# Eight pairs of feature blocks with seven products, and the down projection split into an early and a late part

## The chip, the core and the metric

The kernel runs on one core of one Trainium2 chip. The metric is the device time of one execution in microseconds (us). The kernel before took 1034.69 us (median of 3 runs, 1034.62 to 1034.87).

## What is computed

The reference is one inference step of a decoder layer: two recurrent branches (mLSTM and retention), a gated merge and an output projection, a layer norm, a SwiGLU feed-forward network, and a second layer norm. There are 512 prompt tokens with outputs and 8 running sequences, so the feed-forward part works on 520 token columns; the model is 1024 wide and the feed-forward part 2816.

```python
def swiglu(x, w_gate, w_up, w_down):
    return (jax.nn.silu(x @ w_gate) * (x @ w_up)) @ w_down
...
        mix, ml_s, rt_s = token_mix(x, pos, run, ml_states[l], rt_states[l], w_in[l], b_in[l],
                                    ml_norm_g[l], rt_norm_g[l], w_out[l])
        x = layer_norm(ALPHA * x + mix, ln1_g[l], ln1_b[l])
        x = layer_norm(ALPHA * x + swiglu(x, w_gate[l], w_up[l], w_down[l]), ln2_g[l], ln2_b[l])
```

The 8 sequences also have matrix states (4 heads, two branches: 64 blocks), each of which is decayed, gets an outer product added and is written out.

## The kernel before

**Numbers as pairs.** Every float32 operand of a large matrix product is split into a rounded high part and the rest (`wH`/`wL`, `x1H`/`x1L`, `hH`/`hL`). ScalarE (ACT) rounds, VectorE (DVE) subtracts. A product of two tiles is then three matmuls into PSUM (low by high, high by low, high by high). All arrays are feature-major: tokens lie along the free axis, 520 columns worked as two halves of 260 ("A" and "B").

**Weights** arrive as 154 units of 128x1024 floats through SyncE's DMA queue (`load_units`, L168) into three `raw` buffers. `split_units` makes `wH` and `wL` in three buffers each; `prep` (L196), called in the middle of each step, starts the split of the unit that is used three steps later and then issues the next loads. The last six units have `wH`/`wL` storage of their own beside that: three of them get a `wy` buffer, the other three wait until `wH` is free.

**The order is written by hand.** Each engine works through its own list in the order in which the program issues it. `run_step` (L200) issues the matmuls of one unit (48 matmuls: 8 feature tiles, 3 parts, 2 halves); `run_pair` (L227) those of one half with one or two columns of units. PSUM tiles `pp` come from a pool of two. What reads a finished `pp` (its "evacuation", `drv["evac"]`) is issued at the start of the next group by `flush()`; helpers that have a second stage put it into `pending`, and `tick()` issues it two feature tiles later. A `side` function, called every two feature tiles, adds small work at counted places.

**Feed-forward part.** The first 4 of 22 feature blocks go by halves (`run_pair`), blocks 4 and 5 go as `plain`: a gate step (sigmoid times itself to `gt`) and an up step (times `gt`, split into `hH`, `hL`, row i). Blocks 6 to 13 go as four pairs in `quad` (L1437): two gate steps, then the two up blocks as one 2x2 by 2x2 block product with **seven** products of a quarter of the size instead of eight. Sums of the activations for that (`combine`, L1402) lie in rows 14 to 21 of `hH`/`hL`, which are not yet in use; sums of the weights are made on DVE from `raw` (`sums`), split (`wzH`/`wzL` for the first sum), and the results are put together on DVE (`post`, `times`, `row`). Blocks 14 to 21 are `plain` again.

**Down projection.** 8 output blocks j, 22 feature rows each, in units of 8, 8 and 6 rows. Blocks 0 to 5 go over both halves; blocks 6 and 7 go as a pair over half A, then block 6 over half B, then block 7 over half B, so that the second layer norm of half A runs beside half B. Evacuation: `z = ALPHA*z + pp` and a running sum `Ssum` over blocks. For half B a mean over blocks 0 to 6 is taken early (`seven`, L1617: a product with `ones7`), and what block 7 adds is corrected at the end.

**Beside it**: `upd_at(rate)` (L1326) is called every two feature tiles and starts state blocks at a rate `R` (L1336): a broadcast load `uk`, a load `uC` (3 blocks ahead, 5 buffers), two ACT and two DVE operations, and a store. All of these DMAs are issued by GpSimd (POOL). When all 64 are out, the pool `dq` is released and `kv_load` (L680) loads the saved operands of two heads, whose state products fill TensorE (PE) at the very end.

The start of a step in `run_step`, and the places of small work and the first two products in `quad`:

```python
        if st.first:
            tick()
            flush()
            drv["ps"] = pmain.tile([128, 2, 512], F32, name="pp")
...
        side = each(upd_at(R[2]), at_q({
            0: [sp(0, a, lambda: r0[:, a])],
            3: [sums],
...
            6: [lambda: tt(r0[:, a], r0[:, a], r1[:, b], ALU.add), sp(0, b, lambda: r0[:, a])],
...
        products = [
            (0, a, x(0, tA), aux, post("p1", None, None)),
            (0, b, y(1), aux, post("u", "p1", ALU.add)),
```

Here `sp` splits a half (a or b, 512 columns) of a weight sum, and the second product needs the half that is made in place 6 of 15.

In the layer norm `centre` subtracts the mean (DVE) and squares (ACT), `fold` adds squares (the first three on POOL, the rest on DVE), `token_cols` sums over partitions with small matmuls, `root` takes the power -0.5 on POOL (tile `nr`), and `over_tokens` spreads it with five transposes on PE. `steps(gen, when)` lists at which `side` count each stage is issued.

Of the kernel before, what the change touches and what calls it, by code (L numbers as in the profile page):

```python
# [25 lines left out]
FF = 22  # L26
# [55 lines left out]
def body(nc, tc, a, o):  # L82
# [1487 lines left out]
    for i in range(3):  # L1570
        extra[UL + i] = lambda: (wy.tile([128, 1024], F32R, name="wyH"), wy.tile([128, 1024], F32R, name="wyL"))
    for j in range(6):
        if j == 5:
            assert upd["n"] == len(UPD) and not pending
            dqp.release()
            kvp = tc.alloc_tile_pool(name="kvp", bufs=1)
            kvx = [kv_load(kvp, 0)]
        k0 = 0
        for n in (8, 8, 6):
            ks = [(k0 + i, slice(i * 128, (i + 1) * 128)) for i in range(n)]  # L1580
            run_step(Step(unit, ks, rhs_h, full, k0 == 0, n == 6, ev_d(j)), upd_at(R[4]))
            k0 += n
# [5 lines left out]
    def ev_pair(ps):
        stt(z[:, 6:8, sA], z[:, 6:8, sA], ALPHA, ps[:, :, :260], ALU.mult, ALU.add)
        add_sum(6, sA)  # L1590
        add_sum(7, sA)

# [21 lines left out]
    def seven():  # L1617
# [12 lines left out]
        tail["sq"] = sq  # L1630
# [103 lines left out]
def _pack(inp):  # L1734
# [26 lines left out]
    for i in range(0, FF, 2):  # L1761
        gu = [unit(w[:, 128 * j:128 * (j + 1)]) for j in (i, i + 1) for w in (wgt, wup)]
        units += [gu[n] for n in ((0, 2, 1, 3) if i in QUADS else (0, 1, 2, 3))]
    for j in range(8):
        k0 = 0
        for n in (8, 8, 6):
            units.append(unit(wd[k0 * 128:(k0 + n) * 128, 128 * j:128 * (j + 1)]))
            k0 += n

    units[-6:] = [units[-6 + 3 * (i % 2) + i // 2] for i in range(6)]  # L1770
    cs, dtab, rw, rs = _constants()
# [65 lines left out]
```

## Time and profile before

| | |
|---|---|
| median of 3 runs | 1034.69 us |
| the profiled execution, its own time | 1035.39 us |
| its span (first to last instruction) | 1033.3 us |
| mean granted TensorE clock | 0.999 |
| PE busy | 1024.7 us, 99% |
| DVE / ACT / POOL busy | 640.8 / 480.9 / 255.6 us |
| moved by DMA | 176.64 MB, 171 GB/s on the mean |

In rows of the timeline the first number is the start in us from the span's start, the second the duration, then engine, line and operation, the tiles written and read, and in brackets how long the engine had been idle before and what released it. L101, L104 and L98 are helpers, so groups are told apart by their tiles.

### The profile page before, as it was taken

To read this page: it belongs to the slowest core of one execution; us is meant where nothing else is said; L and a number is where in the kernel's file an instruction comes from. 1 tells how busy PE (TensorE), PEld (TensorE's weight loads), DVE (VectorE), ACT (ScalarE), POOL (GpSimd) and SP (SyncE) were. 2 spreads that over 40 slices of the span, in tenths; PEclk is the share of its full clock that TensorE was granted. 3 is DMA by queue.
4 is the path that set the end of the run, shared out by engine and by line. 5 is a ranking of instruction groups with operands and counts; after the bars stand their busy time and mean duration, and the time that the engine had idled before them with its cause. 6 is when DMAs were issued, how large, how long until landed. Compare 5 with 4: busy or idle time off the path is not lost.

```text
span 1033.3 us, 21326 instructions
## 1 busy us (share of the span) xinstructions
PE 1024.7 (99%) x8506; PEld 1017.9 (99%) x8506; DVE 640.8 (62%) x1423; ACT 480.9 (47%) x960; POOL 255.6 (25%) x431
## 2 busy tenths in 40 slices
PE   9999999999999999999999999999999999999998
PEld 8999999999999999999999999999999999999997
DVE  4747753568555486535595748768888655555345
ACT  5454443554424544435554316645544544444224
POOL 1212302312303232021122135321211333343004
PEclk9999999999999999999999999999999999999999
DMA  6334442544343754422345563364565878888633
GB/s 238 98 130 138 153 154 96 173 143 140 135 143 117 257 164 140 153 96 78 131 150 170 170 227 114 113 222 146 161 208 189 277 258 250 271 291 310 220 110 104
DMA packets 64715, 176.64 MB, mean 171 GB/s; under 512 B 9220, under 2 KB 18948, under 8 KB 64360
## 3 DMA queue, kind: packets, MB, share of 16 engines
q1 hardware_dynamic: 47080, 123.55, 34.7%
q0 software_dynamic: 17536, 51.74, 16.1%
q8 instruction: 67, 1.10, 0.4%
q14 instruction: 32, 0.26, 0.1%
HBM read 146.09 MB, written 27.85 MB: 168 GB/s over the span
## 4 chain that ended last, share of the span: by engine, by line
PE 91%; DVE 4%; issue 1%; ACT 1%; DMA 1%; POOL 1%; SPq 0%; POOLq 0%; DVEq 0%; ACTq 0%
PE pp L220 64%; PE pp L243 11%; PE aux L1541 2%; PE acc L1541 2%; PE aux L586 2%; PE acc L184 1%; PE acc L186 1%; PE acc L185 1%; DVE wL L101 1%; PE aux L184 1%; PE aux L185 1%; PE aux L186 1%; PE pp L350 1%; PE aux L826 1%; ACT wH L98 1%
## 5 line engine op out<-in xcount | busy, mean ns | idle before, releaser
L220 PE MATMUL pp<-xH,wL 128*128 128x260 f32 (+1 forms) x1248 | 259.4, 289 | 0.0
L220 PE MATMUL pp<-xH,wH 128*128 128x260 f32 (+1 forms) x1248 | 252.6, 284 | 0.0
L220 PE MATMUL pp<-xL,wH 128*128 128x260 f32 (+1 forms) x1248 | 252.4, 284 | 0.0
L101 DVE TENSOR_TENSOR wL<-raw,wH 128x1024 fp32r<-128x1024 f32 (+2 forms) x161 | 182.1, 1133 | 68.2 <-ACT wH L98 67.0
L220 PEld LDWEIGHTS pp<-xH,wL 128*128 128x128 f32 x1248 | 193.0, 189 | 0.7
L220 PEld LDWEIGHTS pp<-xH,wH 128*128 128x128 f32 x1248 | 193.0, 188 | 0.0
L220 PEld LDWEIGHTS pp<-xL,wH 128*128 128x128 f32 x1248 | 192.9, 188 | 0.0
L98 ACT ACTIVATE wH<-raw 128x1024 fp32r<-128x1024 f32 (+2 forms) x161 | 155.2, 966 | 42.6 <-PE pp L220 25.0
L220 PE MATMUL pp<-x1H,wL 128*128 128x260 f32 x448 | 90.2, 282 | 0.4 <-DVE gt L101 0.4
L220 PE MATMUL pp<-x1H,wH 128*128 128x260 f32 x448 | 90.3, 283 | 0.0
L220 PE MATMUL pp<-x1L,wH 128*128 128x260 f32 x448 | 90.1, 283 | 0.0
L220 PEld LDWEIGHTS pp<-x1H,wL 128*128 128x128 f32 x448 | 69.1, 189 | 0.7 <-DVE gt L101 0.7
L220 PEld LDWEIGHTS pp<-x1H,wH 128*128 128x128 f32 x448 | 69.1, 188 | 0.0
L220 PEld LDWEIGHTS pp<-x1L,wH 128*128 128x128 f32 x448 | 68.9, 188 | 0.0
L98 ACT ACTIVATE raw<-pp,cols 128x536 f32<-128x536 f32 (+1 forms) x48 | 33.7, 702 | 74.4 <-PE pp L220 69.3
L98 ACT ACTIVATE sq<-uk,vsA 128x256 f32<-128x256 f32 x128 | 56.9, 496 | 20.5 <-DMA uk<-kq3m 9.6
L104 DVE SCALAR_TENSOR_TENSOR dt<-dC,dq 128x256 f32<-128x256 f32 x128 | 57.4, 449 | 2.8 <-DMA dC<-sC 0.3
L220 PE MATMUL pp<-hH,wL 128*128 128x260 f32 x264 | 53.3, 283 | 0.0
L220 PE MATMUL pp<-hH,wH 128*128 128x260 f32 x264 | 53.1, 282 | 0.0
L220 PE MATMUL pp<-hL,wH 128*128 128x260 f32 x264 | 53.1, 282 | 0.0
L101 DVE TENSOR_TENSOR gt<-gt,pp 128x520 f32<-128x520 f32 (+1 forms) x44 | 26.2, 595 | 35.1 <-ACT gt L98 22.6
L98 ACT ACTIVATE tmp<-pp,cols 128x520 f32<-128x520 f32 (+1 forms) x25 | 16.7, 674 | 61.8 <-PE pp L220 61.8
(425 smaller groups left out, 2165.8 us busy)
## 6 DMA issues: line engine op xcount, KB each, us to landing
raw<-wall SPq DMA_DIRECT2D x154, 512.0 KB, 3.8
dC<-sC SPq DMA_DIRECT2D x32, 256.0 KB, 4.3
dC<-sS SPq DMA_DIRECT2D x32, 256.0 KB, 4.2
uC<-sC POOLq DMA_DIRECT2D x32, 256.0 KB, 6.2
dC<-uC POOLq DMA_DIRECT2D x32, 256.0 KB, 4.3
uC<-sS POOLq DMA_DIRECT2D x32, 256.0 KB, 6.0
dS<-uC POOLq DMA_DIRECT2D x32, 256.0 KB, 4.3
raw<-xT SPq DMA_DIRECT2D x8, 268.0 KB, 4.3
```

What stands on the lines that cost most here:

```text
L98: A.activation(out, in_, func, **kw)
L101: (eng or V).tensor_tensor(out, x, y, op=op)
L104: V.scalar_tensor_tensor(out, x, s, y, op0=op0, op1=op1, **kw)
L184: PE.matmul(out, ll, rh, start=start, stop=False)
L185: PE.matmul(out, lh, rl, start=False, stop=False)
L186: PE.matmul(out, lh, rh, start=False, stop=stop)
L220: PE.matmul(ps[:, hi, :wd], w, r[:, lo:lo + wd], start=(st.first and i == 0 and pi == 0), stop=(st.last and i == n - 1 and pi == 2))
L243: PE.matmul(ps[:, hi, :n], w[:, c], r, start=(i == 0 and pi == 0), stop=(i == last and pi == 2))
L350: PE.matmul(first_ps[u][:, hi, :268], w[:, c], r[:, k, hi * 268:(hi + 1) * 268], start=(k == 0 and pi == 0), stop=(k == 7 and pi == 2))
L586: PE.transpose(ps[:m, i * 256 + dt * 128:i * 256 + dt * 128 + 128], src[:, dt, 128 * j:128 * j + m], ident)
L826: PE.transpose(ps[:, 128 * i:128 * (i + 1)], tiles[h]["nat" + br][:, i, et * 128:(et + 1) * 128], ident)
L1541: PE.matmul(ps[:, :260], w[:, s], r, start=(k == 0 and pi == 0), stop=(k == 3 and pi == 2))
```

## The change

Four more pairs go with seven products: `QUADS` now covers blocks 6 to 21, and no block after 5 is `plain`. The sums of the activations must therefore stay in rows 14 to 21 of `hH`/`hL` to the end of block 21. Rows of blocks 14 to 21 are stored in rows 0 to 7 instead (`hrow`), and those are free because the down projection of feature rows 0 to 7 is done early: right after the pair of blocks 8 and 9, eight steps (one for each j, 48 matmuls, one unit) put `z = ALPHA*z + pp`. The down projection after the last pair then has 14 rows left for each j, in units of 6 and 8 rows, and adds `pp` to `z`. Blocks 0 to 4 go over both halves; block 5 now goes alone over half A, blocks 6 and 7 as a pair over half A, then 5, 6 and 7 each over half B. For half B the early mean is over blocks 0 to 5 (`six`, at other counts), and the sum of blocks 6 and 7 (`z67`) is corrected at the end. The rates `R` of the state updates change, so that all 64 are out before block 4 of the down projection.

```diff
-QUADS = range(6, 14, 2)
+QUADS = range(6, 22, 2)
+EARLY = 8
+HR = 14
...
+    def hrow(i):
+        return i if i < HR else i - HR
...
-    R = (0.33, 0.2, 0.19, 0.36, 0.44)
+    R = (0.35, 0.25, 0.21, 0.48, 0.56)
...
-            split(hH[:, i, :], hL[:, i, :], g)
+            split(hH[:, hrow(i), :], hL[:, hrow(i), :], g)
...
     for i in QUADS:
         quad(i)
-    for i in range(QUADS.stop, FF):
-        plain(i, upd_at(R[3]))
-    unit = UF + 2 * FF
+        if i == EARLY:
+            for j in range(8):
+                run_step(Step(UF + 2 * i + 4 + j, kcols, rhs_h, full, True, True, ev_early(j)), upd_at(R[3]))
+    unit = UF + 2 * FF + 8
...
-    for j in range(6):
-        if j == 5:
+    krows = (range(EARLY, HR), range(FF - HR))
+    for j in range(5):
+        if j == 4:
             assert upd["n"] == len(UPD) and not pending
             dqp.release()
             kvp = tc.alloc_tile_pool(name="kvp", bufs=1)
             kvx = [kv_load(kvp, 0)]
...
     split_units(NU - 1)
     load_units(NU)
     split_units(NU)
     drain()
     kvx.append(kv_load(kvp, 1))
-    run_pair(ks, rhs_h, 0, 260, ev_pair)
+    run_pair(down_ks(5), rhs_h, 0, 260, ev_rest(sA, 5))
+    run_pair(down_ks(6, 7), rhs_h, 0, 260, ev_rest(sA, 6, 7))
...
     def ev_six(ps):
-        stt(z[:, 6, sB], z[:, 6, sB], ALPHA, ps[:, 0, :260], ALU.mult, ALU.add)
-        add_sum(6, sB)
+        tt(z[:, 6, sB], z[:, 6, sB], ps[:, 0, :260], ALU.add)
+        sq[6] = bt.tile([128, 260], F32, name="sq", bufs=8)
+        act(sq[6], z[:, 6, sB], AF.Square)
+        tail["z67"] = bt.tile([128, 260], F32, name="sq", bufs=8)
+        tt(tail["z67"], z[:, 6, sB], z[:, 7, sB], ALU.add)
...
-    side = each(steps(lnA, (3, 4, 5, 7, 12, 15, 17)), steps(seven(), (13, 14, 15, 18)))
-    run_pair([(k, ws[:1]) for k, ws in ks], rhs_h, 260, 260, ev_six, side)
+    side = each(steps(lnA, (3, 4, 5, 7, 12, 15, 17)), steps(six(), (8, 9, 11, 15)))
+    run_pair(down_ks(5), rhs_h, 260, 260, ev_rest(sB, 5), side)
+    run_pair(down_ks(6), rhs_h, 260, 260, ev_six, side)
     last_ps = {}
-    run_pair([(k, ws[1:]) for k, ws in ks], rhs_h, 260, 260, lambda ps: last_ps.update(ps=ps), side)
+    run_pair(down_ks(7), rhs_h, 260, 260, lambda ps: last_ps.update(ps=ps), side)
...
     tt(z7, z7, last_ps["ps"][:, 0, :260], ALU.add)
-    sq4 = tail["sq"][4]
+    z67 = tail["z67"]
+    tt(z67, z67, last_ps["ps"][:, 0, :260], ALU.add)
...
-    token_cols(z7, pc)
+    token_cols(z67, pc)
     token_cols(sq7, pv2)
```

On the matmuls the change is a count: PE has 48 matmuls of 260 columns fewer (128x3 fewer in up steps, 7x12 for each of four pairs more). Where instructions change places is seen at three spots.

**DVE at the end of the down projection.** The list of DVE before; `uC` rows are state updates, `wL`/`wyL` rows splits of weight units (the last six are the last six units), `z<-z,pp` with 520 columns the evacuation of a whole output block, `128x2x260` that of the pair 6 and 7 over half A:

```order
L104 SCALAR_TENSOR_TENSOR uC<-uC,sq 128x256 x2
L101 TENSOR_TENSOR wL<-raw,wH 128x1024 x3
L104 SCALAR_TENSOR_TENSOR z<-z,pp 128x520
L101 TENSOR_TENSOR Ssum<-Ssum,z 128x520
L101 TENSOR_TENSOR wL<-raw,wH 128x1024
L101 TENSOR_TENSOR wyL<-raw,wyH 128x1024 x3
L101 TENSOR_TENSOR wL<-raw,wH 128x1024 x3
L104 SCALAR_TENSOR_TENSOR z<-z,pp 128x520
L101 TENSOR_TENSOR Ssum<-Ssum,z 128x520
```

The same place after the change:

```order
L104 TENSOR_TENSOR z<-z,pp 128x520
L104 TENSOR_TENSOR Ssum<-Ssum,z 128x520
L107 SCALAR_TENSOR_TENSOR uC<-uC,sq 128x256 x4
L104 TENSOR_TENSOR wL<-raw,wH 128x1024 x2
L104 TENSOR_TENSOR z<-z,pp 128x520
L104 TENSOR_TENSOR Ssum<-Ssum,z 128x520
L104 TENSOR_TENSOR wyL<-raw,wyH 128x1024 x3
L104 TENSOR_TENSOR wL<-raw,wH 128x1024 x3
L104 TENSOR_TENSOR z<-z,pp 128x520
L104 TENSOR_TENSOR Ssum<-Ssum,z 128x520
L104 TENSOR_TENSOR z<-z,pp 128x260
```

In both lists the last full block is evacuated behind the splits of all six last units; that block is now block 4 instead of 5, with the 260 columns of block 5 behind it, and the last updates stand one block of weights nearer to it: two updates behind the evacuation of block 2, where before one stood behind that of block 3.

**DVE beside half B.** Before; `z<-z,aux` is the subtraction of a mean, `sq<-sq` the folding of squares, `vc` the small column that `root` reads:

```order
L104 SCALAR_TENSOR_TENSOR z<-z,pp 128x2x260
L101 TENSOR_TENSOR Ssum<-Ssum,z 128x260 x2
L101 TENSOR_TENSOR z<-z,aux 128x260 x8
L101 TENSOR_TENSOR sq<-sq 128x260 x4
L104 SCALAR_TENSOR_TENSOR z<-z,pp 128x260
L101 TENSOR_TENSOR Ssum<-Ssum,z 128x260
L110 TENSOR_SCALAR vc<-aux 52x5
L104 SCALAR_TENSOR_TENSOR z<-z,aux 128x260
L101 TENSOR_TENSOR z<-z,aux 128x260 x4
```

And after the change:

```order
L104 TENSOR_TENSOR z<-z,pp 128x2x260
L104 TENSOR_TENSOR Ssum<-Ssum,z 128x260 x2
L104 TENSOR_TENSOR z<-z,aux 128x260 x8
L104 TENSOR_TENSOR z<-z,pp 128x260
L104 TENSOR_TENSOR Ssum<-Ssum,z 128x260
L104 TENSOR_TENSOR sq<-sq 128x260 x4
L104 TENSOR_TENSOR z<-z,aux 128x260 x8
L113 TENSOR_SCALAR vc<-aux 52x5
```

The evacuation of half B's first block moved ahead of the folding for half A, and all eight subtractions for half B moved ahead of `vc` of half A.

**POOL at the same place.** Before; `sq<-sq` is the folding of the first three squares (of half A, then of half B), `nr` the root, `z<-z,rb` the scaling:

```order
L1323 DMA dS<-uC 128x512 x3
L101 TENSOR_TENSOR sq<-sq 128x260 x3
L101 TENSOR_TENSOR nr<-vc,nhalf 52x5
L101 TENSOR_TENSOR sq<-sq 128x260 x3
L101 TENSOR_TENSOR z<-z,rb 128x260 x5
L101 TENSOR_TENSOR nr<-vc,nhalf 52x5
```

And after the change:

```order
L1329 DMA dS<-uC 128x512 x3
L104 TENSOR_TENSOR sq<-sq 128x260 x6
L104 TENSOR_TENSOR nr<-vc,nhalf 52x5
L104 TENSOR_TENSOR z<-z,rb 128x260 x5
L104 TENSOR_TENSOR nr<-vc,nhalf 52x5
```

Half B's three additions now stand ahead of half A's root.

More of the change, by code (lines that the diff above doesn't have):

```diff
@@ L1437, in quad @@
     def quad(i):
-        base = UF + 2 * i
+        base = UF + 2 * i + (8 if i > EARLY else 0)
         load_units(base + 8)
@@ L1514, in row @@
             times(j, s, c)
-            return split_g(hH[:, j, :], hL[:, j, :], gt.pop(j))
+            return split_g(hH[:, hrow(j), :], hL[:, hrow(j), :], gt.pop(j))
         def last():
@@ L1551, in body, with ev_early, go @@
         plain(i, side)
+    def ev_early(j):
+        def go(ps):
+            v3 = z[:, j, :].rearrange("p (a b) -> p a b", a=2)
+            stt(v3, v3, ALPHA, ps[:, :, :260], ALU.mult, ALU.add)
+        return go
     for i in QUADS:
         quad(i)
-    for i in range(QUADS.stop, FF):
-        plain(i, upd_at(R[3]))
-    unit = UF + 2 * FF
+        if i == EARLY:
+            for j in range(8):
+                run_step(Step(UF + 2 * i + 4 + j, kcols, rhs_h, full, True, True, ev_early(j)), upd_at(R[3]))
+    unit = UF + 2 * FF + 8
     wz.release()
@@ L1562, in go @@
             v3 = z[:, j, :].rearrange("p (a b) -> p a b", a=2)
-            stt(v3, v3, ALPHA, ps[:, :, :260], ALU.mult, ALU.add)
+            tt(v3, v3, ps[:, :, :260], ALU.add)
             add_sum(j, slice(0, NQ))
@@ L1577, in body, with down_ks, ev_rest, go @@
             kvx = [kv_load(kvp, 0)]
[L1578 to L1582, printed above, removed]
+        for n, rows in enumerate(krows):
+            ks = [(k, slice(i * 128, (i + 1) * 128)) for i, k in enumerate(rows)]
+            run_step(Step(unit, ks, rhs_h, full, n == 0, n == 1, ev_d(j)), upd_at(R[4]))
             unit += 1
-    ks = [(k, tuple((UL + 2 * (k // 8) + i, slice(k % 8 * 128, k % 8 * 128 + 128)) for i in range(2))) for k in range(FF)]
+    def down_ks(*js):
+        return [(k, tuple((UL + 2 * (j - 5) + n, slice(i * 128, (i + 1) * 128)) for j in js))
+                for n, rows in enumerate(krows) for i, k in enumerate(rows)]
     sA, sB = slice(0, 260), slice(260, NQ)
[L1588 to L1591, printed above, removed]
+    def ev_rest(s, *js):
+        def go(ps):
+            v = z[:, js[0]:js[-1] + 1, s]
+            tt(v, v, ps[:, :len(js), :260], ALU.add)
+            for j in js:
+                add_sum(j, s)
+        return go
     split_units(NU - 1)
@@ L1597, in body @@
     kvx.append(kv_load(kvp, 1))
-    run_pair(ks, rhs_h, 0, 260, ev_pair)
+    run_pair(down_ks(5), rhs_h, 0, 260, ev_rest(sA, 5))
+    run_pair(down_ks(6, 7), rhs_h, 0, 260, ev_rest(sA, 6, 7))
+    sq = {}
     def ev_six(ps):
-        stt(z[:, 6, sB], z[:, 6, sB], ALPHA, ps[:, 0, :260], ALU.mult, ALU.add)
-        add_sum(6, sB)
+        tt(z[:, 6, sB], z[:, 6, sB], ps[:, 0, :260], ALU.add)
[3 more added lines that the diff above has]
+        tt(tail["z67"], z[:, 6, sB], z[:, 7, sB], ALU.add)
     tail = {}
@@ L1612, in fill, with six @@
             next(late_mm, None)
-    ones7 = bt.tile([128, 128], F32, name="ones7")
-    V.memset(ones7, 1.0 / 896)
-    def seven():
+    ones6 = bt.tile([128, 128], F32, name="ones6")
+    V.memset(ones6, 1.0 / 768)
+    def six():
         ps = aux()
-        PE.matmul(ps[:, :260], ones7, Ssum[:, sB], start=True, stop=True)
+        PE.matmul(ps[:, :260], ones6, Ssum[:, sB], start=True, stop=True)
         mean = ps[:, :260]
         yield
-        sq = {}
-        stt(z[:, 7, sB], z[:, 7, sB], ALPHA, mean, ALU.mult, ALU.subtract)
+        for j in (6, 7):
+            tt(z[:, j, sB], z[:, j, sB], mean, ALU.subtract)
         centre(mean, range(0, 4), sB, sq)
@@ L1626, in seven @@
         yield
-        centre(mean, range(4, 7), sB, sq)
+        centre(mean, range(4, 6), sB, sq)
         yield
         fold(sq, (4, 5, 6, 0))
-        tail["sq"] = sq
     lnA = layer_norm(0, ln2_finish)
-    side = each(steps(lnA, (3, 4, 5, 7, 12, 15, 17)), steps(seven(), (13, 14, 15, 18)))
-    run_pair([(k, ws[:1]) for k, ws in ks], rhs_h, 260, 260, ev_six, side)
+    side = each(steps(lnA, (3, 4, 5, 7, 12, 15, 17)), steps(six(), (8, 9, 11, 15)))
+    run_pair(down_ks(5), rhs_h, 260, 260, ev_rest(sB, 5), side)
+    run_pair(down_ks(6), rhs_h, 260, 260, ev_six, side)
     last_ps = {}
-    run_pair([(k, ws[1:]) for k, ws in ks], rhs_h, 260, 260, lambda ps: last_ps.update(ps=ps), side)
+    run_pair(down_ks(7), rhs_h, 260, 260, lambda ps: last_ps.update(ps=ps), side)
     tick()
@@ L1642, in body @@
     tt(z7, z7, last_ps["ps"][:, 0, :260], ALU.add)
-    sq4 = tail["sq"][4]
+    z67 = tail["z67"]
+    tt(z67, z67, last_ps["ps"][:, 0, :260], ALU.add)
+    sq4 = sq[4]
     sq7 = bt.tile([128, 260], F32, name="sq", bufs=8)
@@ L1649, in body @@
     pc = aux()
-    token_cols(z7, pc)
+    token_cols(z67, pc)
     token_cols(sq7, pv2)
     pd = aux()
-    PE.matmul(pd[:, :260], onesD, z7, start=True, stop=True)
+    PE.matmul(pd[:, :260], onesD, z67, start=True, stop=True)
     pd2 = acc()
-    PE.matmul(pd2[:, :260], onesD, z7, start=True, stop=True)
+    PE.matmul(pd2[:, :260], onesD, z67, start=True, stop=True)
     dc = bt.tile([52, 5], F32, name="dc", bufs=1)
@@ L1763, in _pack @@
         units += [gu[n] for n in ((0, 2, 1, 3) if i in QUADS else (0, 1, 2, 3))]
+        if i == EARLY:
+            units += [unit(wd[:EARLY * 128, 128 * j:128 * (j + 1)]) for j in range(8)]
     for j in range(8):
[L1765 to L1770, printed above, removed]
+        for b in (slice(EARLY, HR), slice(HR, FF)):
+            units.append(unit(wd[b.start * 128:b.stop * 128, 128 * j:128 * (j + 1)]))
     cs, dtab, rw, rs = _constants()
```

## The prediction

> **What bounds the kernel now.** I read the page first, then the busy time of the engines by stages, then what PE waited for (asked for the stretch from 590 us to the end).
>
> ```profile
> PE 1024.7 (99%) x8506; PEld 1017.9 (99%) x8506; DVE 640.8 (62%) x1423; ACT 480.9 (47%) x960; POOL 255.6 (25%) x431
> ```
>
> ```profile
> core 0: us, PE busy (x) PEld busy (x) DVE busy (x) ACT busy (x) POOL busy (x), PEclk, DMA share, GB/s
> 732.20:754.00 21.80, 21.80 (x183) 21.80 (x183) 18.13 (x34) 10.44 (x19) 4.27 (x8) 1.00 0.55 168
> 911.00:934.00 23.00, 23.00 (x194) 23.00 (x193) 11.95 (x21) 10.63 (x19) 8.60 (x18) 1.00 0.90 309
> ```
>
> ```profile
> PE aux L1164 <- POOL nr L101: 1.2, 1, 1.2
> PE pp L220 <- DVE gt L101: 0.4, 1, 0.4
> ```
>
> The reader should see that PE never rests: busy throughout both stages (a pair of blocks; the down projection) at full clock, and from 590 us to the end only two waits, 1.6 us in all. The second, 0.4, is at the first pair, where DVE is late with a gate's evacuation; the change leaves it. So the time is PE's work plus a short tail, and a matmul removed is worth its whole spacing, as long as nothing else becomes late. Who is near to being late: DVE during a pair (18.13 of 21.8 us, 83%), and DMA during the down projection (0.90).
>
> **The matmuls removed.** Starts of the first matmul of a pair's seven products, of the next pair's gate steps, and of that pair's products:
>
> ```profile
> 722.18 0.29 PE L1541 MATMUL aux<-x1H,wzL 128*128 128x260 f32 x1
> 732.26 0.40 PE L220 MATMUL pp<-x1H,wL 128*128 128x260 f32 x2
> 743.80 0.29 PE L1541 MATMUL aux<-x1H,wzL 128*128 128x260 f32 x1
> ```
>
> Seven products are 84 matmuls and took 10.08 us; two plain steps are 96 and took 11.54 us: 0.120 us each in both. Four more pairs save 48 x 0.120 = **-5.8 us**. The early down steps move as many matmuls as they take from the end (8 x 48), and each needs one new unit per 48 matmuls like the plain step whose place it takes, so they cost PE nothing by themselves; they do their evacuation in one DVE operation where a gate or up step needs one or two.
>
> **A wait for `pp` before the pair of blocks 6 and 7.** The largest cost, I think. `pp` has two buffers. Block 4 fills one, block 5's half A the other (42 matmuls, 5.04 us), then the pair needs block 4's buffer again. But block 4's evacuation stands on DVE behind the split of the last unit of all, and that unit's load stands on SP behind `kv_load`, which must wait until the last state store has landed (its buffers lie in the released pool). Before, this chain lay beside the pair's own 132 matmuls, which wrote into a buffer that had been free for a whole block. Its times:
>
> ```profile
> 954.46 0.75 DVE L104 SCALAR_TENSOR_TENSOR uC<-uC,sq 128x256 f32<-128x256 f32 x2
> 955.51 0.54 POOL L1323 DMA_DIRECT2D dS<-uC  x1 [2.97 <-DVE uC L104]
> 967.60 0.93 SPq L690 DMA_DIRECT2D kvk<-kvd  x2
> 974.00:976.00 2.00, 2.00 (x19) 2.00 (x18) 0.00 (x0) 0.00 (x0) 0.00 (x0) 1.00 1.01 363
> 983.47 1.06 ACT L98 ACTIVATE wH<-raw 128x1024 fp32r<-128x1024 f32 x1 [0.85 <-DMA raw<-wall]
> 984.74 18.02 PE pp L243 x150
> 986.18 1.06 ACT L98 ACTIVATE wH<-raw 128x1024 fp32r<-128x1024 f32 x1 [1.64 <-DMA raw<-wall]
> 988.41 0.69 DVE L104 SCALAR_TENSOR_TENSOR z<-z,pp 128x520 f32<-128x520 f32 x1
> ```
>
> From the first `kv_load` DMA to the landing of the third unit behind it: 967.60 to 983.47, 15.9 us, with DMA full (1.01). From the last unit's rounding to the end of the evacuation: 986.18 to 989.10, 2.9 us. Before, four units stood behind `kv_load`; now it comes one unit later in SP's order, so three do, and the third is the last. So if `kv_load` starts at s (counted from the start of block 5), the buffer is free at s + 18.8 and PE, there at 5.04, waits s + 13.8.
>
> When is s? A block is now 84 matmuls, 10.08 us, so block 3 starts at -20.2. Before, the update behind an evacuation issued its store 2.4 us after its block's start (block 4 started 264 matmuls before 984.74, at 953.1; store 955.51). Now two updates stand there: 0.7 more, store at -17.1. How long stores and loads took to land, by the page and by the tile `uC` from 700 us on:
>
> ```profile
> dS<-uC POOLq DMA_DIRECT2D x32, 256.0 KB, 4.3
> DMA to landing us min/median/max: 2.3/5.5/10.3
> ```
>
> That gives s from -12.8 (4.3) to -6.8 (10.3), a wait from 1.0 to 7.0. I take s = -11.3, nearer the median, later by 1.5 because the rate rises from 0.44 to 0.56 where DMA was 0.90 busy already: **+2.5 us**.
>
> In the Trainium skill (DMA: Bandwidth & Descriptors, section Where 436 GB/s comes from) HBM gives one core some 358 GB/s: the 3.7 MB of `kv_load` and three units would then need 10.5 us instead of 15.9, the wait would go and the sum below would be 2.5 us lower. The trace reached 363 GB/s in two microseconds of that stretch, but not over all of it.
>
> **Two waits beside half B.** The stages of half A's norm against half B's, before:
>
> ```profile
> 1000.43 0.28 PE L243 MATMUL pp<-hH,wyL 128*128 128x260 f32 x1
> 1002.76 0.44 PE aux L1172 x2
> 1003.24 2.77 DVE L101 TENSOR_TENSOR z<-z,aux 128x260 f32<-128x260 f32 x8 [0.98 <-PE aux L1172]
> 1004.53 2.46 POOL L101 TENSOR_TENSOR sq<-sq 128x260 f32<-128x260 f32 x3 [48.48 <-ACT sq L98]
> 1005.92 2.43 DVE L101 TENSOR_TENSOR sq<-sq 128x260 f32<-128x260 f32 x4
> 1008.96 0.42 DVE L104 SCALAR_TENSOR_TENSOR z<-z,pp 128x260 f32<-128x260 f32 x1 [0.61 <-PE pp L243]
> 1009.42 0.43 DVE L101 TENSOR_TENSOR Ssum<-Ssum,z 128x260 f32<-128x260 f32 x1
> 1009.64 0.57 PE aux L1158 x10
> 1010.49 1.19 POOL L101 TENSOR_TENSOR nr<-vc,nhalf 52x5 f32<-52x5 f32 x1 [3.49 <-DVE vc L110]
> ```
>
> I count from the start S of half B (1000.43 before). Up to the subtractions (S+2.8 to S+5.6) nothing changes. After the change block 5's half B ends on PE at S+5.5 (42 matmuls and the mean's 0.44); evacuation and sum take 0.9 (1008.96 to 1009.85), from S+5.7 to S+6.6. The product with `ones6` is due at place 8, S+6.2: **+0.45 us** with the hop. DVE then folds (1.9 to 2.4, to S+8.5) and does eight subtractions (2.8). The first two of those are for blocks 6 and 7, so the second square comes after four of them (1.4) and its own 0.4: POOL's fold for half B starts at S+10.4 and takes 2.46: S+12.9. Only then comes half A's root (1.19): S+14.1. The transposes stand at place 15, which PE reaches at S+12.8 (90 matmuls 10.8, mean products 0.88, columns 0.57, the wait 0.45, hops): **+1.2 us**. In the order before, the root came ahead of that fold, so it cost nothing.
>
> **The end.** What follows the last matmul:
>
> ```profile
> 1018.64 0.57 PE acc L1158 x10
> 1018.68 0.42 DVE L101 TENSOR_TENSOR z<-z,pp 128x260 f32<-128x260 f32 x1 [0.21 <-PE pp L243]
> 1019.20 0.61 PE L1158 MATMUL aux<-ones,z 128*52 128x1 f32 x10
> 1020.76 1.17 POOL L101 TENSOR_TENSOR nr<-vc,nhalf 52x5 f32<-52x5 f32 x1 [1.00 <-DVE vc L104]
> ```
>
> The columns on `aux` began 0.10 after the addition to `z7`. They now need `z67`, one DVE addition later (0.35, 2.77/8): **+0.35 us**, and everything up to the root follows.
>
> **Less slack in each pair.** The second product needs the half of `wzL` that DVE writes just before it. First and last pair before:
>
> ```profile
> 722.00 0.69 DVE L101 TENSOR_TENSOR wzL<-raw,wzH 128x512 fp32r<-128x512 f32 x1 [0.70 <-ACT wzH L98]
> 723.62 0.28 PE L1541 MATMUL aux<-hH,wzL 128*128 128x260 f32 x1
> 787.50 0.69 DVE L101 TENSOR_TENSOR wzL<-raw,wzH 128x512 fp32r<-128x512 f32 x1 [0.70 <-ACT wzH L98]
> 788.49 0.28 PE L1541 MATMUL aux<-hH,wzL 128*128 128x260 f32 x1
> ```
>
> The slack fell from 0.93 to 0.30 us over three pairs, 0.21 a pair: the chain of DVE and ACT is slower than PE. Now six pairs follow each other, and in DVE's order two updates instead of one (0.75 each, 954.46) stand ahead of that half in four of the eight. From 0 to 2 us; I take **+0.8**, some 0.2 for each of those four. The early steps run updates at 0.48 instead of 0.36, close to the 0.44 of the stretch 911 to 934 where PE did not wait, but with a buffer every 5.7 us: 0 to 2 us, I take **+0.4**.
>
> **Sum**: -5.8 + 2.5 + 0.45 + 1.2 + 0.35 + 0.8 + 0.4 = -0.1 us on the profiled execution's 1035.39 us (span 1033.3). The median of the runs is 0.70 lower, and I set the change against it: **1034.6 us**, no change. About 0.2% (2.1 us) is what a measurement of this kernel can tell from no change.
>
> **Rivals.**
>
> *Faster.* The transfers come in time: stores land in 4.3 us (wait 1.0), pairs and early steps hide their updates (0, 0). -5.8 + 1.0 + 2.0 = -2.8: 1031.9 us; without any wait for `pp`, 1030.9. For it: PE waited for nothing in comparable stretches. Against it: slack of 0.30, DMA at 0.90. Chance 0.29.
>
> *Slower.* The last state store lands late. From s = -9.1 on (8.0 us after issue) the wait is 4.7 and the sum passes +2.1. At s = -8 the wait is 5.8: +3.2, 1037.9 us. For it: updates are asked for 1.27 times as fast as in the stretch at 0.90, and a landing of 10.3 was seen. Against it: the last loads are issued three updates ahead, so that stretch ends quieter. Chance 0.18.
>
> *The clock falls in the `pp` wait.* After PE's last matmul the granted clock fell within 5 us, and at the start it took PE from 1.25 to 6.26 us to reach its pace:
>
> ```profile
> 1030.00:1033.30 3.30, 0.00 (x0) 0.00 (x0) 0.00 (x0) 0.00 (x0) 0.00 (x0) 0.55 0.32 105
> 1.25 3.36 PE L334 MATMUL aux<-ones 128*128 128x128 f32 x14 [1.25 <-DVE onesR L157]
> 6.26 0.45 PE L350 MATMUL pp<-xH,wH 128*128 128x268 f32 x2
> ```
>
> Five microseconds at half pace cost 2.5: 1037.1 us. The wait of 1.2 in the table above had no such effect. The Trainium skill (TensorE: Matmul & The Clock Gate, section HAM oscillation — how this bites in real kernels) puts the limit at a gap of some 3.4 us; by that rule my 2.5 is safe and a wait of 4 would not be. Chance 0.06.
>
> *Not fewer matmuls*, or DVE the bound in every pair: the first is excluded by the count in the order, the second would cost 0.2 to 0.4 in each of eight pairs, 1036 to 1038 us. Chance 0.02.
>
> **How the numbers follow.** No change 0.45 (its own range 1032.6 to 1036.7), faster 0.29, slower 0.18 + 0.06 + 0.02 = 0.26. The range goes down to 1031.2, past the faster case's 1031.9 but not to 1030.9, and up to 1037.7, short of the late store's 1037.9; about 1 in 10 lies beyond each end.
>
> **What would show it.** Right: PE's waits list a wait for DVE's `z<-z,pp` of 1 to 4 us just before block 6 and 7's pair, one of about 1.2 for POOL's `nr` and one of about 0.4 for `Ssum`; the products' rows stay 0.120 apart. Wrong: no PE wait over 0.5 us after the last pair of feature blocks (then 1030 to 1031 us), `kvk` issued later than 9 us before block 5, or PE waits spread over the pairs.

## The result and the profile after

The changed kernel took 1045.11 us (median of 4 runs, 1044.10 to 1045.99) beside 1034.65 us of the kernel before on the same chip: ratio 1.0099, 95% interval 1.0088 to 1.0111. It is slower by 10.5 us where the forecast was 1034.6 us with a range up to 1037.7. The profiled execution took 1044.1 us, its span is 1042.4 us (before 1033.3).

The list of what PE waited for, from 560 us to the end (us in all, times, longest):

```profile
PE pp L223 <- DVE wL L104: 4.4, 2, 2.7
PE pp L246 <- DVE z L104: 3.7, 1, 3.7
PE aux L1167 <- POOL nr L104: 2.2, 2, 1.2
PE pp L223 <- DVE gt L104: 1.7, 1, 1.7
PE aux L1643 <- DVE Ssum L104: 0.5, 1, 0.5
PE aux L1161 <- DVE sq L104: 0.4, 1, 0.4
```

Before there were two, 1.6 us in all (one of the two for `nr`, at 630 us, is one of them). The waits for `z`, `nr` and `Ssum` and the 0.4 at the end are the ones that the prediction lists. The first row is new: PE waits twice in the down projection for the low half of a weight unit. This is where it comes from, in the timelines of the engines, by time (at the end of a row: how long the engine stood idle, and for what):

```profile
960.70 0.55 POOL L1329 DMA_DIRECT2D dS<-uC  x1 [0.92 <-DVE uC L107]
961.24 0.54 POOL L1313 DMA_DIRECT2D uk<-kq3r  x1
968.42 1.71 ACT L101 ACTIVATE sq<-uk,vsA 128x256 f32<-128x256 f32 x4 [4.53 <-DMA uk<-kq3r]
970.04 1.99 ACT L101 ACTIVATE wH<-raw 128x1024 fp32r<-128x1024 f32 x2
972.68 0.76 DVE L107 SCALAR_TENSOR_TENSOR uC<-uC,sq 128x256 f32<-128x256 f32 x2 [1.92 <-ACT wH L101]
973.36 2.35 DVE L104 TENSOR_TENSOR wL<-raw,wH 128x1024 fp32r<-128x1024 f32 x2
973.73 0.54 POOL L1329 DMA_DIRECT2D dS<-uC  x1 [2.13 <-DVE uC L107]
974.72 0.77 PE L223 MATMUL pp<-hH,wL 128*128 128x260 f32 x2 [2.70 <-DVE wL L104]
976.42 0.93 SPq L693 DMA_DIRECT2D kvk<-kvd  x2
989.76 1.06 ACT L101 ACTIVATE wH<-raw 128x1024 fp32r<-128x1024 f32 x1 [7.04 <-DMA raw<-wall]
994.43 0.69 DVE L104 TENSOR_TENSOR z<-z,pp 128x520 f32<-128x520 f32 x1
995.18 0.59 PE L246 MATMUL pp<-hH,wyL 128*128 128x260 f32 x1 [3.72 <-DVE z L104]
```

Read it from the top. POOL asks for the key rows `uk` of a later update only after the store of the one before, and that store waits for DVE. The rows land late (asked for at 961.24, used at 968.42); ACT, which takes its list in order, stands 4.53 us for them while `wH` of two units waits behind; DVE's `wL` follows, and PE last. The last state store goes out at 973.73, so `kv_load` starts at 976.42, 9.8 us before block 5 (986.25), the last three units are rounded from 989.76 on, and block 4's evacuation stands behind their splits.

ACT waited for key rows before the change too. The view of the tile `uk` from 900 to 990 us says who waited for it (us in all, times), before and after:

```profile
  ACT sq L98: 12.9, 5
  ACT sq L101: 18.6, 5
```

Before, none of that reached PE: there were no waits in the down projection. So the order of asking is old, and PE waits for it only in the changed kernel, at 0.56 instead of 0.44.

The second loss stands in the granted clock (the columns as in the prediction: length, busy times, PEclk, DMA share, GB/s). After the wait of 2.70, after that of 3.72, and in the last stretch:

```profile
974.00:976.00 2.00, 1.28 (x6) 1.31 (x7) 2.00 (x3) 0.00 (x0) 0.28 (x1) 0.59 0.47 147
976.00:978.00 2.00, 2.00 (x12) 2.00 (x12) 1.97 (x3) 0.00 (x0) 0.00 (x0) 0.56 0.91 272
...
994.00:996.00 2.00, 0.82 (x4) 0.82 (x5) 1.97 (x4) 0.00 (x0) 0.00 (x0) 0.71 0.96 307
996.00:998.00 2.00, 2.00 (x11) 2.00 (x11) 0.77 (x3) 0.00 (x0) 0.00 (x0) 0.50 1.00 304
998.00:1000.00 2.00, 2.00 (x18) 2.00 (x17) 0.00 (x0) 0.00 (x0) 0.00 (x0) 0.94 0.96 378
```

```profile
1028.40:1030.40 2.00, 2.00 (x11) 1.69 (x10) 1.73 (x5) 2.00 (x5) 1.91 (x3) 0.64 0.55 186
1030.40:1032.40 2.00, 2.00 (x11) 1.90 (x12) 1.37 (x5) 1.03 (x3) 1.37 (x2) 0.50 0.46 151
```

What is missing from 1.00, times the 2 us, over the half that is missing while the clock is at half: (0.41 + 0.44) x 2 / 0.5 = 3.4 us at half clock, (0.29 + 0.50 + 0.06) x 4 = 3.4, (0.36 + 0.50) x 4 = 3.4. Where PE has work in such a stretch it does half of it: some 1.4 to 1.5 us each.

**The balance**, span 1033.3 to 1042.4, +9.1: matmuls -5.8; waits for `wL` 4.4 and half clock behind them 1.5; wait for `z` 3.7 and half clock 1.5; first pair 1.2 (1.67 now, 0.44 before); `Ssum` 0.5, `nr` 0.9; the end 1.8 (of it some 1.4 half clock); and -1.4 since code that did not change reached the same row (transposes of `nr`) at 629.79 instead of 631.22. That is 8.3; the other 0.8 is about what five new waits leave out: each is counted from the end of PE's last matmul, 0.28 us after its start, where the next could have begun 0.12 after it, so 0.16 each. The -1.4 need not come from the change: in the twelve other traces of changed kernels that row stands between 630.1 and 631.3.

### The profile page after: what moved, and what is told of

Its sections match the earlier page's. It is cut to its first block, busy times and chain, and to the rows that moved or that the text cites. A ratio compares the mean times of both kernels' runs of the same rounds, so it can differ in the third digit from the quotient of the medians.

```text
span 1042.4 us, 21347 instructions
## 1 busy us (share of the span) xinstructions
PE 1022.8 (98%) x8458; PEld 1015.6 (97%) x8458; DVE 673.3 (65%) x1506; ACT 490.7 (47%) x984; POOL 255.7 (25%) x431
## 3 DMA queue, kind: packets, MB, share of 16 engines
q0 software_dynamic: 17536, 51.74, 15.9%
## 4 chain that ended last, share of the span: by engine, by line
PE 86%; DMA 4%; DVE 4%; ACT 2%; issue 2%; POOL 1%; SPq 0%; POOLq 0%; DVEq 0%; ACTq 0%
PE pp L223 57%; PE pp L246 10%; PE aux L1547 4%; PE acc L1547 3%; PE aux L589 2%; PE acc L187 2%; PE acc L189 1%; PE acc L188 1%; DMA raw<-wall 1%; DVE wL L104 1%; PE aux L187 1%; ACT wH L101 1%; PE aux L188 1%; PE aux L189 1%; PE pp L353 1%
## 5 line engine op out<-in xcount | busy, mean ns | idle before, releaser
L101 ACT ACTIVATE wH<-raw 128x1024 fp32r<-128x1024 f32 (+2 forms) x173 | 159.0, 922 | 34.5 <-DVE raw L104 15.5
L223 PE MATMUL pp<-x1H,wL 128*128 128x260 f32 x320 | 64.5, 282 | 1.7 <-DVE gt L104 1.7
L223 PE MATMUL pp<-x1H,wH 128*128 128x260 f32 x320 | 64.5, 283 | 0.0
L223 PE MATMUL pp<-x1L,wH 128*128 128x260 f32 x320 | 64.4, 283 | 0.0
L223 PEld LDWEIGHTS pp<-x1H,wL 128*128 128x128 f32 x320 | 49.3, 189 | 1.9 <-DVE gt L104 1.9
L223 PEld LDWEIGHTS pp<-x1H,wH 128*128 128x128 f32 x320 | 49.3, 188 | 0.0
L223 PEld LDWEIGHTS pp<-x1L,wH 128*128 128x128 f32 x320 | 49.2, 188 | 0.0
L223 PEld LDWEIGHTS pp<-hH,wL 128*128 128x128 f32 x268 | 41.9, 191 | 4.8 <-issue 4.8
```

The lines of the kernel that those rows point to most:

```text
L101: A.activation(out, in_, func, **kw)
L223: PE.matmul(ps[:, hi, :wd], w, r[:, lo:lo + wd], start=(st.first and i == 0 and pi == 0), stop=(st.last and i == n - 1 and pi == 2))
```

## The experiments

All times are medians beside the kernel before on the same chip (1034.7 to 1034.9 us). "The changed kernel" is that of the forecast, 1045.1 us.

**1. Without the last 16 updates.**

```diff
-    UPD = [(h, br, b) for h in range(H) for br in "mr" for b in range(NB)]
+    UPD = [(h, br, b) for h in range(H) for br in "mr" for b in range(NB)][:48]
```

> The changed kernel without the last 16 of the 64 state updates (their states are neither loaded nor stored), so that none is left for the down projection. Theory U (the updates crowd into blocks 0 to 3 of the down projection; ACT waits there for their key rows and the rounding of weights stands behind it; the last store is late and with it the loads for the pair of blocks 6 and 7): both waits for wL (1.72, 2.70) and the 3.72 for z go, and with them the two stretches at half clock (1.44, 1.5): 1045.1 - 4.4 - 1.4 - 3.7 - 1.5 = 1034.1 us. Theory T (the new order of the tail's norms is what costs): 1045 us, as the tail is untouched. Theory D (the wait for pp is made by DVE's order, not by late transfers): the weight waits go, the 3.72 stays: 1039.3.

Measured: 1034.09 us, ratio 0.9994 (0.9985 to 1.0003). PE's waits:

```profile
PE aux L1167 <- POOL nr L104: 2.1, 2, 1.2
PE pp L223 <- DVE gt L104: 1.7, 1, 1.7
PE aux L1643 <- DVE Ssum L104: 0.5, 1, 0.5
PE aux L1161 <- DVE sq L104: 0.4, 1, 0.4
```

Both large rows are gone, the small ones are as they were. So the 11 us hang on these updates; the tail's new order (theory T) is not the main cost. It also shows that the tail and the first pair eat most of the 5.8 us by themselves.

**2. Block 4's evacuation first.**

```diff
+    tick()
+    flush()
     split_units(NU - 1)
```

> Block 4's evacuation is put on DVE ahead of the last units' splits. Theory U (transfers late): the wait for z goes, but the pair of blocks 6 and 7 then waits for its own weights, whose split ends about 993.3 on the changed kernel's scale against a start at 991.3: some 2.0 us for wyL in place of 3.72, too short to halve the clock: -1.7 - 1.5, 1041.9 us; the two weight waits in blocks 0 to 4 stay at about 1.7 and 2.7. Theory D (only the order on DVE): the wait goes altogether, -5.2: 1039.9. If the half clock has nothing to do with the wait's length: 1043.4.

Measured: 1042.24 us, ratio 1.0074 (1.0062 to 1.0086).

```profile
PE pp L223 <- DVE wL L104: 5.3, 2, 3.6
...
PE pp L246 <- DVE wL L104: 0.2, 1, 0.2
```

The wait for `z` is gone and only 0.2 of the 2.0 for the weights came in its place, so DVE's order was needed for it; run 6 shows that the late loads were too. The waits for `wL` took 0.9 more in this execution, and the half clock behind them lasted 6.8 us instead of 3.4, about 1.5 more; that kept the time above 1039.9.

**3. Updates earlier.**

```diff
-    R = (0.35, 0.25, 0.21, 0.48, 0.56)
+    R = (0.35, 0.25, 0.27, 0.52, 0.25)
```

> The rates at which updates are started become 0.27 in the pairs (was 0.21), 0.52 in the early down steps (0.48) and 0.25 in the down projection (0.56): the same work, moved ahead. Theory U: the weight waits and most of the wait for z go, with the half clock behind them: 1045.1 - 11 = 1034 us, in the range 1033 to 1036. Theory P (DVE is the bound in the eight pairs, an update more in each costs PE its 0.75 us or a good part): waits of 0.3 to 0.8 in each pair, +2 to +6, so 1036 to 1040. Theory T: 1045 or above.

Measured: 1042.04 us, ratio 1.0068 (1.0056 to 1.0080). My theory's 1034 fails, and so does P's 1036 to 1040:

```profile
PE pp L223 <- DVE z L107: 3.6, 2, 2.3
...
PE aux L1547 <- DVE wzL L104: 1.7, 4, 0.6
...
PE pp L246 <- DVE z L104: 0.6, 1, 0.6
```

The waits for `wL` went, but others came: in the early steps for the evacuation into `z` (1.23 and 2.35), and in four of the pairs for `wzL` (0.23 to 0.60). The rows of the first kind, from ACT and DVE:

```profile
790.33 1.70 ACT L101 ACTIVATE sq<-uk,vsA 128x256 f32<-128x256 f32 x4 [4.95 <-DMA uk<-kq1r]
...
791.72 0.76 DVE L107 SCALAR_TENSOR_TENSOR uC<-uC,sq 128x256 f32<-128x256 f32 x2 [5.09 <-ACT sq L101]
792.40 0.69 DVE L107 SCALAR_TENSOR_TENSOR z<-z,pp 128x520 f32<-128x520 f32 x1
```

The same chain again, at another place: key rows late, ACT waits, DVE's update waits for ACT, and what PE needs stands behind it. Moving updates moves the wait.

**4. Half A's root first.**

```diff
-    side = each(steps(lnA, (3, 4, 5, 7, 12, 15, 17)), steps(six(), (8, 9, 11, 15)))
+    side = each(steps(lnA, (3, 4, 5, 7, 10, 15, 17)), steps(six(), (8, 10, 11, 15)))
```

> The columns and the root of half A's norm stand two places earlier (10 in place of 12) and half B's subtractions and fold one later (10 in place of 9), so that POOL has the root before the fold. Prediction's step (the root behind the fold): the wait for nr of 0.94 becomes under 0.2, everything else as it was: 1044.1 to 1044.3 us, in the measurement's noise. Theory T (the tail's order is the main cost, the fall of the clock at the end included): -0.9 - 1.4, 1042.8 or less.

Measured: 1044.00 us, ratio 1.0088 (1.0075 to 1.0101). The wait for `nr` beside half B is gone (the row is 1.2, once: the one at 630 us), as the prediction's step would have it. The end ran at full clock here; but it did so in five traces that still had this wait, so the one does not hang on the other. The time tells nothing: the runs lie between 1040.98 and 1046.22, and waits elsewhere differ from the changed kernel's trace (5.1 for `wL`, 2.6 for `z`, 2.1 in the early steps).

**5. Filler matmuls.**

```diff
+    ps = aux()
+    for n in range(20):
+        PE.matmul(ps[:, :260], wH[UL][:, 0:128], hH[:, 0, sA], start=(n == 0), stop=(n == 19))
     run_pair(down_ks(6, 7), rhs_h, 0, 260, ev_rest(sA, 6, 7))
```

> Twenty matmuls of 260 columns that nothing reads (2.4 us) are put on PE just before the pair of blocks 6 and 7, where the changed kernel waited 3.72 us. If the half clock behind that wait comes from PE having nothing to do for so long: the wait that is left is some 1.3 us, the products behind it stay 0.120 us apart, and the time is 1.5 us lower in spite of 20 matmuls more, about 1043.6. If the clock falls for another reason: the stretch at half clock stays and the time is 1045 or above.

Measured: 1042.44 us, ratio 1.0078 (1.0066 to 1.0090). The wait for `z` is no longer listed, the row of the pair's first matmul is 0.33 us late, and the products behind it are 0.120 apart. The clock stayed, as expected; but this run does not show that the filler kept it. PE came to block 5 at 989.27, 3.0 us later than in the changed kernel, after a wait of 4.16 for `wL` with 6.8 us at half clock, so that the filler stood in for a wait of 2.7 us (994.31 to 997.03), and behind the 2.60 of run 4 the clock held without filler. The last section has what the traces say of the cause.

**6. kv's loads behind the last units.**

```diff
-            kvx = [kv_load(kvp, 0)]
...
-    kvx.append(kv_load(kvp, 1))
+    kvx = [kv_load(kvp, i) for i in range(2)]
```

> The first kv_load stands on SP behind the last units of weights instead of ahead of the last three. Theory U (the wait for z hangs on the last unit's load, which stands behind kv_load, which waits for the last state store): the 3.72 and the half clock behind it go, 1045.1 - 3.7 - 1.5 = 1039.9 us; the waits for wL stay. Theory D (order on DVE alone, the loads have nothing to do with it): 1045.

Measured: 1040.49 us, ratio 1.0055 (1.0041 to 1.0070). The wait for `z` is gone with DVE's order untouched: it needed the late loads as well (theory U, 1039.9). The waits for `wL` stayed:

```profile
PE pp L223 <- DVE wL L104: 5.1, 2, 3.6
```

**7. Key rows first.** The load of `uk` for the update three further on is issued right after ACT's part of an update, ahead of the store.

```diff
         if n < len(UPD):
             h, br, b = UPD[n]
-            if b % 2 == 0:
-                upd["k"] = dqp.tile([128, 512], F32, name="uk", bufs=2)
...
             act(t[et], k, AF.Copy, scale=vsA[:, 2 * h + (br == "r"), et, b:b + 1])
+        uk_load(n + 3)
         yield
...
```

> Each update issues its load of the next key rows ahead of its own store on POOL's queue (not behind it, where the store waits for DVE). Theory O (the weights are late because of the order: the key rows are asked for too late): the row comes 1 to 2 us earlier, ACT's waits for uk shrink by as much, the two waits for wL fall below 3 us together and the clock stays up: 1042 us. Theory B (DMA is full: an update is 256 KB in, 256 KB out and 128 KB of key rows, 655 thousand bytes; 0.56 of it in 1.44 us and a unit of 524 thousand in 5.04 us are 359 GB/s, where 300 to 338 were moved): the backlog is the same, waits for wL of 4 to 5 us together, 1044.5 to 1045.5.

Measured: 1041.66 us, ratio 1.0067 (1.0055 to 1.0079).

```profile
PE pp L246 <- DVE z L104: 5.0, 1, 5.0
...
PE pp L223 <- DVE wL L104: 1.0, 2, 0.6
```

The waits for `wL` fell from 4.4 to 1.0 with the same data in the same stretch. Theory B, which I held by then, is wrong on this: it was the order of asking. The wait for `z` grew, as PE came to it sooner, and 6.8 us at half clock followed it: that the clock would stay up was wrong.

**8. Updates over five blocks.** `kv_load` as in run 6, and the pool `dq` is released there too, behind the last splits; the updates may then run through block 4.

```diff
-    R = (0.35, 0.25, 0.21, 0.48, 0.56)
+    R = (0.35, 0.25, 0.21, 0.44, 0.46)
```

> The loads of kv stand behind the last units, and so the updates may run through block 4 too: rate 0.44 in the early steps (was 0.48) and 0.46 over five blocks (0.56 over four); all 64 are done. Theory B (DMA full above some 320 GB/s): the demand falls from 359 to 313 GB/s in the down projection and from 309 to 291 in the early steps, so the waits for wL go or stay under 1 us together, the wait for z goes, and the half clock with them: 1034 us, in the range 1033 to 1036, as without the last 16 updates. Theory N (updates in the down projection cost what they cost, however they are spread): a wait for wL in each of five blocks, 1040 or above.

Measured: 1038.28 us (9 runs, 1034.37 to 1039.59), ratio 1.0025 (1.0014 to 1.0036). The profiled execution was the quickest, with no wait for `wL` but 2.06 for `z`. The others show a mean clock of 0.995 to 1.000, so that waits came and went between executions. Between the theories: spreading helps, but does not make it safe.

**9. First rates back.**

```diff
-    R = (0.35, 0.25, 0.21, 0.48, 0.56)
+    R = (0.33, 0.2, 0.218, 0.48, 0.56)
```

> The first two rates are set back to 0.33 and 0.20 (changed kernel 0.35 and 0.25), the third raised from 0.21 to 0.218 so that all 64 updates are still done. If the first pair's wait for the gate's evacuation (1.67 us, before 0.44) comes from the update that these rates put on DVE just ahead of it: it falls to 0.4 to 0.9 and the time by some 1 us, to 1044 us. If PE merely comes there 1.4 us earlier than it did before, and DVE is what sets that place: the wait stays at 1.5 to 1.8, 1045. The other waits stay as they are in both.

Measured: 1042.55 us, ratio 1.0075 (1.0061 to 1.0088).

```profile
PE pp L223 <- DVE gt L104: 0.5, 1, 0.5
```

The first pair's wait is that of before again, so the rates made it: 1.2 us of the 2.6. The rest is not: the trace has one wait for `wL` instead of two, by chance or by the shifted updates; these runs cannot tell. My expectation that the other waits stay was wrong.

**10. Only the two orders** (runs 6 and 7 together; all rates as in the changed kernel).

> Only two orders of loads are changed: the key rows are asked for ahead of the store (as in the run with that alone), and kv's loads stand behind the last units (as in the run with that alone). The updates keep the changed kernel's rates and stretch: 0.56 over four blocks. Theory O (the order in which loads are asked for made the waits, not the amount of data): waits for wL of 1 us together, no wait for z, no half clock: 1045.1 - 4.75 - 1.44 - 3.9 - 1.5 + 1.0 = 1034.5 us, in the range 1033.5 to 1036. Theory B (the stretch holds more data than DMA carries, the spread over five blocks is what mended it): waits for wL or wyL of 3 us or more, 1038 or above.

Measured: 1035.62 us (11 runs), ratio 1.0006 (0.9997 to 1.0015).

```profile
PE pp L223 <- DVE gt L104: 1.7, 1, 1.7
PE pp L223 <- DVE wL L104: 1.1, 2, 0.7
...
```

The wait for `z` is gone. Nothing is left out and no rate is changed, and 9.5 of the 10.5 us are gone. That settles it for theory O against B: at these rates, the loads were asked for in an order that made ACT, DVE and then PE wait. (The rate was needed as well: with the old order at 0.44, in the kernel before, and at 0.46, in the profiled execution of run 8, PE does not wait for `wL`.)

**11 and 12. All mends together**, in two divisions of the updates. Beside the edits of runs 2, 4, 7 and 8:

```diff
-    R = (0.35, 0.25, 0.21, 0.48, 0.56)
+    R = (0.33, 0.2, 0.22, 0.45, 0.43)
...
-    side = each(steps(lnA, (3, 4, 5, 7, 12, 15, 17)), steps(six(), (8, 9, 11, 15)))
+    side = each(steps(lnA, (3, 4, 5, 7, 10, 15, 17)), steps(six(), (9, 10, 11, 15)))
...
-    tt(z7, z7, last_ps["ps"][:, 0, :260], ALU.add)
     z67 = tail["z67"]
     tt(z67, z67, last_ps["ps"][:, 0, :260], ALU.add)
+    tt(z7, z7, last_ps["ps"][:, 0, :260], ALU.add)
```

> All mends together, nothing left out: updates over five blocks (rates 0.33, 0.20, 0.22, 0.45, 0.43), kv's loads behind the last units, key rows asked for ahead of the store, block 4's evacuation ahead of the last splits, half A's root two places earlier, half B's mean one place later, and the addition to z67 ahead of that to z7. If the terms that the single edits showed add up: no wait for wL, under 0.5 us for z or wyL, no half clock, no wait for nr, 0.4 to 0.9 at the first pair: before's 1034.7 less 5.8 for the matmuls, with 0.5 to 1.5 left over, 1029.5 to 1031 us, faster than both kernels. If the load of DMA and DVE finds another place to wait at: 1033 or above.

> As the run with all mends, but with more updates in the pairs (0.235 instead of 0.22) and fewer behind them (0.43 and 0.40). Theory P (in the pairs DVE has hardly any slack: at 0.27 each pair cost 0.2 to 0.8): waits for wzL of 0.1 to 0.3 in the later pairs, 0.5 to 1.5 us over the other. If there is slack up to 0.235: the same time or 0.5 lower, with less backlog in the down projection.

Measured: 1029.44 us, ratio 0.9952 (0.9939 to 0.9964), and 1030.48 us, ratio 0.9961 (0.9948 to 0.9973). The first is faster than before by 5.5 us and than the changed kernel by 15.7. Its waits, with those of the stretch that was slow:

```profile
PE aux L1167 <- POOL nr L104: 1.2, 1, 1.2
PE aux L1161 <- DVE sq L104: 0.5, 1, 0.5
PE pp L223 <- DVE gt L104: 0.4, 1, 0.4
PE acc L1161 <- ACT dc L101: 0.2, 1, 0.2
```

```profile
940.00:950.00 10.00, 10.00 (x86) 10.00 (x84) 5.99 (x10) 3.44 (x7) 4.85 (x9) 1.00 1.01 348
950.00:960.00 10.00, 10.00 (x86) 10.00 (x85) 5.85 (x11) 5.57 (x11) 4.83 (x9) 1.00 1.00 352
960.00:970.00 10.00, 10.00 (x86) 10.00 (x85) 5.76 (x11) 6.66 (x12) 2.71 (x5) 1.00 0.95 348
```

DMA carries 348 to 352 GB/s here for 30 us and PE never waits: the 300 to 338 that I had taken for full were not. With 0.235 in the pairs a wait for `wzL` of 0.39 came back in one of them; that division is no better, and the two intervals overlap. One mend brought nothing to be seen: with the addition to `z67` first, PE's end still took as long as with it second (10.22 us from the last product of the down projection in this trace and in run 4's, 9.91 before).

## Why the prediction was wrong, point by point

- **Matmuls removed, -5.8: right.** Products stayed 0.120 apart at full clock, and run 11 brings 5.5 of it home.
- **Wait for `pp`, +2.5: mechanism right, size off.** The formula s + 13.8 with the measured s = -9.8 gives 4.0; 3.72 was measured. The mis-sized term is s (-11.3): the store did not land late (2.7 us, 973.73 to 976.42), it was issued 4.6 us late, at 973.73, 12.5 us before block 5 instead of 17.1. The other terms held: 15.8 us from `kv_load` to the rounding of the last unit (976.42 to 992.20; 15.9 in the sum) and 2.9 to the end of the evacuation. But "with DMA full (1.01)" was read off two microseconds; over the whole stretch before, 967.60 to 983.47, the share was 0.83 at 276 GB/s.
- **The step that failed**: "later by 1.5 because the rate rises from 0.44 to 0.56 where DMA was 0.90 busy already". That 1.5 us was all I charged for the higher rate in the down projection, to the one load behind the last store. An update's late key rows also hold up what stands behind them on ACT and DVE, the weights of the next step: 4.4 us of waits and 1.5 of half clock that the sum did not have, and the 4.6 us by which the store was late. Run 7 shows it: with only the order of asking changed, the waits for weights fell from 4.4 to 1.0. I had asked only what waits for DMA, not what waits behind the waiting instruction.
- **The clock, 0.06 and only for the wait for `pp`: wrong.** It fell in three places in this execution, 4.4 us together, and in other runs behind waits of 2.35 and 2.79 us; it held behind 2.06, 2.10 and 2.60. By the Trainium skill's rule that I quoted (TensorE: Matmul & The Clock Gate, section HAM oscillation — how this bites in real kernels), a wait of 2.5 was safe; the trace of the changed kernel, with the half clock behind 2.70, disagrees.
- **"The change leaves it" (first pair): wrong**, +1.2. I had listed the new rates but not looked at the first two of them; run 9.
- **`Ssum` +0.45, `nr` +1.2, `z67` +0.35: right**: 0.48, 0.94, 0.37.
- **Less slack in the pairs +0.8, early steps +0.4: zero in this trace.** Run 3 shows that both are real at a little more: at 0.27 the pairs wait 0.23 to 0.60, at 0.52 the early steps 1.23 and 2.35. Run 4, with the changed kernel's rates, had a wait of 2.10 in the early steps, so that one is not safe at 0.48 either.
- **Rivals.** The late store (0.18; s = -9.8 is between my 1037.9 case and my own) came half true. No case of mine went above 1038 us, since none had PE wait for weights. All that I had named as signs of being right came (3.72 for `z`, 0.94 for `nr`, 0.48 for `Ssum`), and no sign of being wrong: they tested only the terms that the sum already had.

## What to carry to other kernels

When optional work is packed into a shorter stretch, ask for each of its waits what else stands behind it on the same in-order engine, and price that, not only the work's own end. Ask for an operand before the instruction that has to wait (here: the next key rows ahead of the store), and put loads that nobody needs soon behind those that somebody does; here these two orders were worth 9.5 us, more than the arithmetic saved. The clock adds to a long wait of PE: of the eleven waits of 2.35 us or more in these traces, ten were followed by half clock, which cost 1.5 us or more, and none of those up to 2.10 was.

## What the runs showed of the hardware

**The half clock comes in pieces of one length.** Apart from the start and the end of each trace it fell in 15 places: behind ten waits, and in the last stretch of five of the 13 executions of a changed kernel (waits and pauses there are below 1 us each; the cost is 1.4 us, 11.66 against 10.27 from the last product of the down projection to PE's end). Each time the stretch at half clock was 3.4 or 6.8 us long: 6.8 behind waits of 3.58, 3.72, 4.16, 4.25 and 5.01, 3.4 behind 2.35, 2.70, 2.79, 3.57 and the changed kernel's 3.72.

The traces show more than lengths. From the clock's first rise on, every stretch between two of its changes, at full clock too, is a whole multiple of 3.413 us in all 14 traces (in the changed kernel 969.39 us, which is 284 of them, then 1, 5, 1, 9, 1 and 2). So each trace can be cut into slots of this length. In run 4, four slots in a row at its wait of 3.72 (from 975.07), then the two in which its wait of 2.60 lies (from 996.69), and in run 3 the slot with the wait of 2.35:

```profile
974.22:977.63 3.41, 0.85 (x8) 0.64 (x6) 0.88 (x3) 1.84 (x2) 0.23 (x1) 1.00 0.30 117
977.63:981.04 3.41, 2.25 (x10) 2.28 (x11) 3.38 (x5) 0.00 (x0) 0.54 (x1) 0.50 0.58 162
981.04:984.46 3.42, 3.42 (x18) 3.42 (x17) 2.11 (x3) 1.06 (x1) 0.00 (x0) 0.50 0.95 315
984.46:987.87 3.41, 3.41 (x30) 3.41 (x30) 1.52 (x2) 1.06 (x1) 0.00 (x0) 1.00 1.01 349
...
994.70:998.11 3.41, 1.99 (x17) 1.78 (x15) 3.12 (x3) 2.12 (x2) 0.00 (x0) 1.00 0.31 81
998.11:1001.52 3.41, 2.23 (x18) 2.23 (x19) 2.74 (x6) 0.00 (x0) 0.00 (x0) 1.00 0.99 303
```

```profile
789.82:793.23 3.41, 1.06 (x10) 0.85 (x8) 1.37 (x3) 2.65 (x5) 0.45 (x1) 1.00 1.02 414
```

PE was busy for 0.25 of the first slot and 0.31 of the last, and half clock followed both; the 2.60 is split between two slots of 0.58 and 0.65, and the clock held. The same over all slots of all traces, with matmuls of fewer than 100 columns left out of the busy time: in front of every fall the share is 0.45 or less (0.42 in the last stretch of the five), in front of every slot that stayed at full clock 0.49 or more. So, as far as these traces go, it is not the length of a wait that counts, but whether it leaves one slot less than about half full; an estimate from these bounds is that a wait of under 1.7 us never does and one of over 3.8 always. Once at half, the clock stayed there behind shares of 0.54 to 0.80, the second piece of 3.4, and rose behind 0.81 or more. That the small matmuls do not count is inferred: with them the slots in front of those five falls would be 0.89 busy. The Trainium skill (TensorE: Matmul & The Clock Gate, section What's actually happening) has some 3.4 us as the length of the idle window that lowers the clock; the slots here have that length, but a slot that was half idle was enough.

**DMA had more to give than the stretch before showed**: 0.90 busy and 309 GB/s there, 352 GB/s at a share of 1.00 in run 11, and 414 GB/s over the 3.4 us of run 3 above. A share of 0.90 was not a limit.
